# A sliding-window matmul: row blocks of w that shrink to 3, 2 and 1 rows per partition, the last two summed together, and a column-group tail of 4 k tiles

## The chip, the cores and the metric

One core of a Trainium2 chip runs the kernel. The metric is device time in microseconds (us), the median of several executions; the profile is one execution. "Span" is the time from the first to the last instruction of that execution, about 1.9 us less than its device time. All runs compared here are of the state "fast" unless it is said otherwise; a run is called slow when it takes over 1.5% longer than the fastest of the same kernel. Engines in the profile: PE (matmul), PEld (its weight load), DVE (vector), ACT (scalar), POOL (GpSimd, which here does little but issue DMAs), SP (sync).

## The reference

```python
# x: (4, 4096, 4096) fp32, w: (4096, 4096) fp32, offsets: 4 integers
for b in range(4):
    o = int(offsets[b])
    out[b] = x[b, o:o+64] @ w        # fp32 (4, 64, 4096)
```

Four windows of 64 rows make 256 rows, two groups (g = 0, 1) of 128. Each of the 4096 x 4096 weights is needed once: 67.1 MB of w, 4.2 MB of x, and 4.2 MB of result. A "k tile" is 128 rows of w, 2.10 MB; there are 32.

## The kernel before

w comes from HBM in fp32 and is cast to fp16 by the DMA on its way into the on-chip memory. Tiles 0 and 1 are loaded apart. Then come "row blocks": one transfer loads r tiles, and each partition gets r whole rows that lie side by side in w. Three buffers of 4 tiles each take turns. The last tiles are the "tail": they come in two column groups of 2048 columns, the second half of the columns first, so that one half of the result is complete, and can be stored, before all of w is there. A "run" is what a transfer reads in one piece for one partition: r rows of 16 KB in a row block, at most 8 KB in the tail. The matmuls add up in PSUM, the memory of eight "banks" that PE writes; adding a bank to the sums in acc is called an evacuation.

```python
    blocks = [(0, 1), (1, 1), (2, 4), (6, 4), (10, 4), (14, 4), (18, 3), (21, 3)]   # (first k tile, rows per partition)
    k_tail = 24
    n_fine = 2
    R_MAX = 4
    wc_pool = ctx.enter_context(tc.tile_pool(name="wc", bufs=3))
    ...
    for k0, r in blocks[2:]:
        t = wc_pool.tile([P, R_MAX * N], fp16, name="wc", tag="wc")
        nc.gpsimd.dma_start(
            out=t[:, : r * N],
            in_=w[k0 * P : (k0 + r) * P, :].rearrange("(p r) n -> p (r n)", r=r),
        )
    ...
    order = [1, 0]                                  # column groups: second half first
    for ng, st in zip(order, (steps, fine_steps)):  # steps: 2 tiles x 2048 columns each; fine_steps: the last piece cut in 3
        t = wc_pool.tile([P, R_MAX * N], fp16, name="wc", tag="wc")
        for ki, n, c0, c1 in st:
            nc.gpsimd.dma_start(...)                # runs of 8 KB in w
    ...
    whole_rows([0, 1], range(8), True)              # per block: sum its tiles in a PSUM bank, then add the bank to acc (DVE)
    for k0, r in blocks[2:-1]:
        whole_rows(range(k0, k0 + r), range(8), False)
    ...                                             # the last block: first column half alone here,
    ng = order[0]                                   # second half together with the tail
    kts = list(last_block) + list(range(k_tail, n_k))
    ...                                             # matmuls, then 4 adds on DVE, 4 copies on ACT and 4 adds of the copies
        store(nc.gpsimd, g, ng * NG, (ng + 1) * NG) # 1 MB each, two of them
    ng = order[1]
    ...                                             # the tail of the first half; stores of 512 KB each, two on ACT's queue, two on SP's
```

## Time and profile before

| | before |
|---|---|
| median (range) | 182.37 us (182.19 to 182.54, 6 runs) |
| span of the profile (that execution took 182.56 us, more than any of the six) | 180.6 us |
| PE, DVE, ACT busy | 125.7, 80.5, 16.5 us |
| moved by the DMAs over the span | 418 GB/s |
| last landing of w; last landing of a store | 169.81; 179.70 us |

The last row is from the trace's completion records, in which each of the 16 DMA engines tells when its share of a transfer is done; I give the time of the last of the 16.

### The profile page before, as it was taken

The page shows a single profiled execution, that of the slowest core. Times are in us where ns is not written, and L with a number is a line of the kernel's source. Part 1 is how long each engine was busy: PE and PEld are TensorE (multiplying, and loading weights), DVE is VectorE, ACT ScalarE, POOL GpSimd, SP SyncE. Part 2 cuts the span into 40 slices and gives each one's busy share as a digit, 9 for nine tenths or more (in the row PEclk, how much of TensorE's full clock was granted, in tenths as well). Part 3 has the DMA queues.
Part 4 walks back from the last instruction along what each step waited for, and adds up shares of the span by engine and source line. Part 5 has one row for each costly group of instructions (what it writes and reads, how often), then busy time and mean ns, then how long its engine had stood idle before and what let it go on. Part 6 is the DMA issues. An engine that isn't in the chain of part 4 may idle for free.

```text
span 180.6 us, 1505 instructions
## 1 busy us (share of the span) xinstructions
PE 125.7 (70%) x576; PEld 58.1 (32%) x576; DVE 80.5 (45%) x120; ACT 16.5 (9%) x23; POOL 14.5 (8%) x29
## 2 busy tenths in 40 slices
PE   0000779504999399808995699999399999987900
PEld 0000774101444144303442244444044444433400
DVE  0000657500578278802876168899374000820460
ACT  2412446500000000000000000000000000400000
POOL 4600000000000100000001000050500100020000
PEclk9999999965799999996999889999879999999996
DMA  5999989999999899999989989999999999999994
GB/s 178 321 256 212 281 181 196 236 232 232 225 218 218 174 210 234 236 218 232 210 181 203 245 191 245 194 239 196 191 212 213 215 216 214 212 216 206 370 419 196
DMA packets 4952, 40.98 MB, mean 227 GB/s; under 512 B 466, under 2 KB 466, under 8 KB 3282
## 3 DMA queue, kind: packets, MB, share of 16 engines
q0 software_dynamic: 4080, 36.70, 93.8%
q1 hardware_dynamic: 432, 2.10, 3.2%
q10 hardware_dynamic: 434, 2.10, 2.8%
q8 instruction: 4, 0.07, 0.1%
q14 instruction: 2, 0.02, 0.0%
HBM read 71.30 MB, written 4.19 MB: 418 GB/s over the span
## 4 chain that ended last, share of the span: by engine, by line
DMA 63%; PE 26%; issue 3%; DVE 2%; POOL 1%; POOLq 1%; DVEq 0%
DMA wc<-in_w_dram 63%; PE bank L144 26%; DVE acc L154 2%; POOL wc L108 1%; POOLq L70 1%; POOL xrow L77 0%; DVEq L251 0%; POOL identity masks.py:197 0%; POOLq L77 0%; POOL w L66 0%; POOLq masks.py:199 0%; DVEq L154 0%; POOLq L240 0%
## 5 line engine op out<-in xcount | busy, mean ns | idle before, releaser
L144 PE MATMUL bank<-wc,xT 128*128 128x512 f16 x480 | 111.6, 396 | 26.2 <-DMA wc<-in_w_dram 26.2
L154 DVE TENSOR_TENSOR acc<-acc,bank 128x512 f32<-128x512 f32 x100 | 67.0, 686 | 70.7 <-PE bank L144 70.0
L144 PEld LDWEIGHTS <-xT 128*128 128x128 f16 x512 | 51.5, 101 | 93.1 <-DMA wc<-in_w_dram 26.7
L130 PE MATMUL bank<-identity,xrow 128*128 128x128 f16 x64 | 7.1, 312 | 20.0 <-DMA xrow<-in_x_dram 20.0
L139 DVE CAST xT<-bank 128x512 f16<-128x512 f32 x8 | 5.5, 692 | 21.9 <-PE bank L130 21.9
L130 PEld LDWEIGHTS <-xrow 128*128 128x128 f16 x64 | 6.7, 149 | 20.2 <-issue 20.2
L200 ACT COPY tmp<-bank 128x512 f32<-128x512 f32 x4 | 2.1, 600 | 119.9 <-PE bank L144 119.9
L89 POOL DMA_DIRECT2D wc<-in_w_dram x6 | 3.2, 542 | 88.2 <-PE bank L144 88.2
L108 POOL DMA_DIRECT2D wc<-in_w_dram x10 | 6.7, 683 | 36.0 <-PE bank L144 26.4
L144 PE MATMUL bank<-w,xT 128*128 128x512 f16 x32 | 7.2, 382 | 0.0
L169 DVE COPY acc<-bank 128x512 f32<-128x512 f32 x8 | 5.5, 692 | 1.4 <-PE bank L144 1.2
L141 ACT CAST xT<-bank 128x512 f16<-128x512 f32 x8 | 4.7, 586 | 8.2 <-PE bank L130 8.2
L171 ACT COPY acc<-bank 128x512 f32<-128x512 f32 x8 | 4.7, 586 | 2.3 <-PE bank L144 2.3
L189 POOL DMA_DIRECT2D out_dram<-acc x2 | 1.1, 534 | 18.1 <-DVE acc L205 18.1
L205 DVE TENSOR_TENSOR acc<-acc,tmp 128x512 f32<-128x512 f32 x4 | 2.5, 681 | 0.0
L63 ACT CAST w<-acc 128x2048 f16<-128x2048 f32 x1 | 1.9, 1897 | 4.9 <-DMA acc<-in_w_dram 4.9
L77 POOL DMA_DIRECT2D xrow<-in_x_dram x4 | 2.1, 523 | 2.1 <-issue 2.1
L62 ACT CAST w<-acc 128x2048 f16<-128x2048 f32 x1 | 1.9, 1897 | 3.0 <-DMA acc<-in_w_dram 3.0
L62 ACT ACT_TABLE_LOAD x1 | 1.3, 1283 | 1.8 <-PEq L240 1.8
L66 POOL DMA_DIRECT2D w<-in_w_dram x1 | 0.7, 660 | 0.8 <-POOLq L240 0.8
masks.py:199 POOL TENSOR_SCALAR_AFFINE_SELECT identity<-identity 128x128 f16<-128x128 f16 x1 | 0.3, 287 | 0.1
masks.py:197 POOL MEMSET identity<- 128x128 f16 x1 | 0.2, 223 | 0.0
(4 smaller groups left out, 0.4 us busy)
## 6 DMA issues: line engine op xcount, KB each, us to landing
wc<-in_w_dram POOLq DMA_DIRECT2D x4, 4096.0 KB, 48.2
wc<-in_w_dram POOLq DMA_DIRECT2D x7, 1024.0 KB, 27.5
wc<-in_w_dram POOLq DMA_DIRECT2D x2, 3072.0 KB, 36.1
xrow<-in_x_dram POOLq DMA_DIRECT2D x4, 512.0 KB, 14.7
out_dram<-acc POOLq DMA_DIRECT2D x2, 1024.0 KB, 14.5
acc<-in_w_dram SPq DMA_DIRECT2D x1, 1024.0 KB, 5.3
w<-in_w_dram POOLq DMA_DIRECT2D x1, 1024.0 KB, 12.2
acc<-in_w_dram ACTq DMA_DIRECT2D x1, 1024.0 KB, 11.5
```

What stands on the lines that cost most here:

```text
L62: nc.scalar.copy(out=w_one[0][:, :NG], in_=w0_32[:, :NG])
L77: nc.gpsimd.dma_start(out=x16[g][m * WIN : (m + 1) * WIN, :], in_=x[b][bass.ds(o, WIN), :],)
L89: nc.gpsimd.dma_start(out=t[:, : r * N], in_=w[k0 * P : (k0 + r) * P, :].rearrange("(p r) n -> p (r n)", r=r),)
L108: nc.gpsimd.dma_start(out=t[:, pos : pos + n * wd].rearrange("p (t n) -> p t n", t=n), in_=w[ki * P : (ki + n) * P, ng * NG + c0 : ng * NG ...
L130: nc.tensor.matmul(out=ps[t][:, i * P : (i + 1) * P], lhsT=x_cols(g, 4 * t + i), rhs=identity[:], start=True, stop=True,)
L139: nc.vector.tensor_copy(out=dst, in_=ps[t][:])
L141: nc.scalar.copy(out=dst, in_=ps[t][:])
L144: nc.tensor.matmul(out=ps[bank][:], lhsT=xT[g][:, kt * P : (kt + 1) * P], rhs=rhs, start=start, stop=stop,)
L154: nc.vector.tensor_add(out=dst, in0=dst, in1=ps[bank][:])
L169: nc.vector.tensor_copy(out=acc[g][:, c * NT : (c + 1) * NT], in_=ps[bank][:])
L171: nc.scalar.copy(out=acc[g][:, c * NT : (c + 1) * NT], in_=ps[bank][:])
L205: nc.vector.tensor_add(out=dst, in0=dst, in1=tmp[2 * g + j // 2][:])
```

## The change

Its intent: the more of w comes as whole rows, the less comes in the short runs of the tail; and if the blocks get smaller towards the end, PE is left with less to do when the last block lands, so that a tail of only 4 tiles is enough to have half of the result stored in time. The blocks of 2 and 1 rows share one buffer and are summed together in PSUM (the "join", one evacuation instead of two), and the whole tail fits one buffer.

```diff
-    blocks = [(0, 1), (1, 1), (2, 4), (6, 4), (10, 4), (14, 4), (18, 3), (21, 3)]
-    k_tail = 24
+    blocks = [(0, 1), (1, 1), (2, 4), (6, 4), (10, 4), (14, 4), (18, 4), (22, 3), (25, 2), (27, 1)]
+    n_join = 2
+    k_tail = 28
...
+    free = 0
     for k0, r in blocks[2:]:
-        t = wc_pool.tile([P, R_MAX * N], fp16, name="wc", tag="wc")
+        if free < r:
+            t = wc_pool.tile([P, R_MAX * N], fp16, name="wc", tag="wc")
+            free = R_MAX
+        base = (R_MAX - free) * N
+        free -= r
...
+    t = wc_pool.tile([P, R_MAX * N], fp16, name="wc", tag="wc")
+    pos = 0
     for ng, st in zip(order, (steps, fine_steps)):
-        t = wc_pool.tile([P, R_MAX * N], fp16, name="wc", tag="wc")
-        pos = 0
...
-    for k0, r in blocks[2:-1]:
+    for k0, r in blocks[2:-n_join]:
         whole_rows(range(k0, k0 + r), range(8), False)
-    (first half of the last block with whole_rows)
+    join = range(blocks[-n_join][0], k_tail)
...
+    def columns(ng, kts):            # matmuls of kts for one column group, then the adds and copies as before
+        ...
+    columns(order[1], list(join))
     ng = order[0]
+    columns(ng, list(join) + list(range(k_tail, n_k)))
```

More of the change, by code (lines that the diff above doesn't have):

```diff
@@ L86 @@
     }
+    free = 0
     for k0, r in blocks[2:]:
-        t = wc_pool.tile([P, R_MAX * N], fp16, name="wc", tag="wc")
+        if free < r:
[3 more added lines that the diff above has]
+        free -= r
         nc.gpsimd.dma_start(
-            out=t[:, : r * N],
+            out=t[:, base : base + r * N],
             in_=w[k0 * P : (k0 + r) * P, :].rearrange("(p r) n -> p (r n)", r=r),
@@ L93 @@
         for q in range(r):
-            src[k0 + q] = lambda a, e, t=t, c=q * N: t[:, c + a : c + e]
+            src[k0 + q] = lambda a, e, t=t, c=base + q * N: t[:, c + a : c + e]
     tail = {}
@@ L173 @@
     whole_rows([0, 1], range(8), True)
-    for k0, r in blocks[2:-1]:
+    for k0, r in blocks[2:-n_join]:
         whole_rows(range(k0, k0 + r), range(8), False)
-    k0, r = blocks[-1]
-    last_block = range(k0, k0 + r)
-    whole_rows(last_block, range(order[1] * n_sub, (order[1] + 1) * n_sub), False)
+    join = range(blocks[-n_join][0], k_tail)
     def tail_mm(ki, g, ng, j, start, stop):
@@ L189, in store @@
             eng.dma_start(out=out_rows[g * P + a : g * P + e, c0:c1], in_=acc[g][a:e, c0:c1])
-    ng = order[0]
-    kts = list(last_block) + list(range(k_tail, n_k))
-    for ki in kts:
-        for g in range(G):
-            for j in range(n_sub):
-                tail_mm(ki, g, ng, j, ki == kts[0], ki == kts[-1])
-    for g in range(G):
-        for j in range(0, n_sub, 2):
-            add_out(4 * g + j, g, ng * n_sub + j)
-            nc.scalar.copy(out=tmp[2 * g + j // 2][:], in_=ps[4 * g + j + 1][:])
-    for g in range(G):
-        for j in range(1, n_sub, 2):
-            c = ng * n_sub + j
-            dst = acc[g][:, c * NT : (c + 1) * NT]
-            nc.vector.tensor_add(out=dst, in0=dst, in1=tmp[2 * g + j // 2][:])
+    def columns(ng, kts):
+        for ki in kts:
+            for g in range(G):
+                for j in range(n_sub):
+                    tail_mm(ki, g, ng, j, ki == kts[0], ki == kts[-1])
+        for g in range(G):
+            for j in range(0, n_sub, 2):
+                add_out(4 * g + j, g, ng * n_sub + j)
+                nc.scalar.copy(out=tmp[2 * g + j // 2][:], in_=ps[4 * g + j + 1][:])
+        for g in range(G):
+            for j in range(1, n_sub, 2):
+                c = ng * n_sub + j
+                dst = acc[g][:, c * NT : (c + 1) * NT]
+                nc.vector.tensor_add(out=dst, in0=dst, in1=tmp[2 * g + j // 2][:])
+    columns(order[1], list(join))
+    ng = order[0]
+    columns(ng, list(join) + list(range(k_tail, n_k)))
+    for g in range(G):
         store(nc.gpsimd, g, ng * NG, (ng + 1) * NG)
```

## The prediction

> **What bounds the kernel now.** I read the page of the kernel before in this order: the bytes, the row of busy slices, the chain that ended last, then the timeline from 60 us on.
>
> ```profile
> span 180.6 us, 1505 instructions
> ...
> DMA  5999989999999899999989989999999999999994
> ...
> HBM read 71.30 MB, written 4.19 MB: 418 GB/s over the span
> ...
> DMA wc<-in_w_dram 63%; PE bank L144 26%; DVE acc L154 2%; POOL wc L108 1%; POOLq L70 1%; POOL xrow L77 0%; DVEq L251 0%; POOL identity masks.py:197 0%; POOLq L77 0%; POOL w L66 0%; POOLq masks.py:199 0%; DVEq L154 0%; POOLq L240 0%
> ```
>
> The DMA row never falls below 8 between the first slice and the last. The whole span, start and end included, moves 71.30 + 4.19 = 75.49 MB at 418 GB/s. PE is busy 70% (and its modelled matmuls flatter it), DVE 45%. The 26% of the chain that is put on PE is not a bound by itself; it must be asked whether DMA was idle meanwhile. The stretches of the trace say no (columns: PE, PEld, DVE, ACT, POOL busy; clock; DMA share; GB/s written by the DMAs, where the weights count half, as they turn from fp32 into fp16 on the way):
>
> ```profile
> 60.00:80.00 20.00, 13.99 (x64) 6.19 (x64) 11.03 (x17) 0.00 (x0) 0.60 (x2) 1.00 0.98 211
> 145.00:165.00 20.00, 18.07 (x84) 8.03 (x82) 4.89 (x8) 2.06 (x4) 1.07 (x2) 1.00 1.06 213
> 165.00:175.00 10.00, 6.91 (x32) 2.94 (x30) 4.87 (x8) 0.00 (x0) 0.00 (x0) 1.00 1.05 353
> ```
>
> So 211 to 213 GB/s written means some 422 to 426 GB/s read. The timeline gives the pace, because PE or the issuing engine starts as each piece lands:
>
> ```profile
> 62.31 13.99 PE L144 MATMUL bank<-wc,xT 128*128 128x512 f16 x64 [3.07 <-DMA wc<-in_w_dram]
> ...
> 81.75 15.62 PE L144 MATMUL bank<-wc,xT 128*128 128x512 f16 x64 [5.46 <-DMA wc<-in_w_dram]
> ...
> 101.13 26.03 PE L144 MATMUL bank<-wc,xT 128*128 128x512 f16 x112 [3.76 <-DMA wc<-in_w_dram]
> ...
> 117.10 2.83 POOL L108 DMA_DIRECT2D wc<-in_w_dram  x4 [18.90 <-PE bank L144]
> 127.47 2.12 POOL L108 DMA_DIRECT2D wc<-in_w_dram  x3 [7.54 <-PE bank L144]
> 130.18 29.12 PE L144 MATMUL bank<-wc,xT 128*128 128x512 f16 x128 [3.02 <-DMA wc<-in_w_dram]
> ...
> 158.35 0.54 POOL L189 DMA_DIRECT2D out_dram<-acc  x1 [17.45 <-DVE acc L205]
> ...
> 164.84 7.07 PE L144 MATMUL bank<-wc,xT 128*128 128x512 f16 x32 [1.27 <-DMA wc<-in_w_dram]
> ...
> 172.08 2.72 SPq L189 DMA_DIRECT2D out_dram<-acc  x2
> ```
>
> A k tile is 128 rows of w, 2.10 MB. Between the landings at 62.31 and 130.18 lie the row blocks of 4, 4, 3 and 3 tiles: 67.87 / 14 = **4.85 us a tile**. Between 130.18 and 164.84 lie seven tail pieces of the size of one tile: 34.66 / 7 = **4.95 us**. One piece's worth is left after 164.84 (the fine pieces), about 5.0 us, so w ends near 169.8. Then 4.19 MB of stores at 418 GB/s take 10.0 us: 179.8. The span ends at 180.6. The end is thus the end of a queue of bytes that never runs dry, and not the chain from the last matmul: all the stores stand behind the last piece of w whatever PE does, so long as they are issued in time.
>
> **What the Trainium skill says.** (1) "DMA: Bandwidth & Descriptors", section Issuing engines are not separate DMA queues: DMAs of all issuing engines run on the same 16 engines and interleave. The trace agrees: its completion records have the four last stores (512 KB each, issued from two engines) land 1.25 us apart, one after the other, at 419 GB/s in all. (2) The same page, section Bandwidth, Measured: 425 GB/s for one 16 MB load, with a ceiling of 435 that it puts on the SBUF side. Here the reads run at 422 to 426 with only half the bytes on the SBUF side; so I take the figure as the limit of what can be read, and there is no large reserve. The page's fixed 2 us a DMA is not seen between queued DMAs, whose landings lie 4.85 or 4.95 us apart. (3) "TensorE: Matmul & The Clock Gate", section HAM oscillation: PE gaps of over some 3.4 us return the clock to half. The trace agrees: 64 matmuls take 13.99 us after a 3.07 us gap (the stretch from 60 to 80 shows a clock of 1.00) and 15.62 us after one of 5.46.
>
> **The change part by part.**
> Bytes: none removed or added. The blocks become 4,4,4,4,4,3,2,1 instead of 4,4,4,4,3,3, and the tail in column groups falls from 8 tiles to 4. Four tiles move from 4.95 to 4.85 us: 4 x 0.10 = **0.4 us earlier**. If the 2- and 1-row blocks run only at the tail's pace, 3 x 0.10 of that is lost.
>
> Evacuations: before, 5 blocks x 16 + 8 + 4 + 8 = 100 adds out of PSUM, 4 adds from tmp, 4 copies. After, 6 x 16 + 4 + 4 + 8 = 112, 8 and 8. DVE gets 12 x 0.686 + 4 x 0.681 = 11.0 us more, ACT 4 x 0.60 = 2.4 us. All of it lies beside transfers, except two changes of column group where banks must come free. The matmuls stay at 512.
>
> Buffers: the fifth block still waits for the first buffer in turn; the blocks of 2 and 1 share one buffer, and the whole tail shares the next. Predicted landings at 4.85 a tile from 101.1: block (18,4) 120.5; (22,3) 135.0; (25,2) 144.7; (27,1) 149.6; tail A, second group's columns, 154.5 and 159.5; tail B 164.4; the fine pieces to 169.4. The issue of (25,2) and (27,1) waits for the matmuls of (14,4), near 117 as now; the queue then holds until 135.0. The issue of all tail pieces waits for the matmuls of (18,4): 120.5 + 15.6 = 136.1; the queue holds until 149.6. So 13 us to spare: DMA doesn't run dry.
>
> PE: from 120.5 on it has 64 matmuls (15.6 us with the cold start, to 136.1), 48 for (22,3) at 0.217 us (to 146.5), 24 for the join's first group (to 151.9, as (27,1) lands at 149.6), then, once banks are free, 56 of the second group, then 32 of the last. At the switch DVE frees a bank in 0.69 us and ACT in 0.60, four each: 2.8 us for eight banks, of which 1.5 us lie under the last matmuls of the join and 1.7 beside the next ones: a stall of some 0.5 us, twice. So the second group ends at 152.4 + 12.2 = 164.6 (before: 155.7), and all matmuls at 165.1 + 7.0 = 172.1 (before: 171.9). PE has nearly no rest from 120.5 on, whereas before it caught up with the DMA at 159.3.
>
> Stores: the first two were issued 2.7 and 3.9 us after the end of the second group (155.7 to 158.35 and 159.56); they come at 167.3 and 168.5, instead of 11 us ahead of the end of w now only 1 to 2 us ahead of 169.4. Still in time. They give the DMA 5 us of work, to 174.4, and the first half of the last group is stored from about 171.1 on. The last store needs its turn near 178 and is issued near 174.8. So the end is again the queue: 169.4 + 10.0 + 0.8 = 180.2, and the sum is **0.4 us less**: 182.35 - 0.4 = **181.95 us**.
>
> **The rivals.**
> (a) PE becomes the bound. For it: 224 matmuls in one run of 51 us ending with the DMA; if the clock stays cold longer or a bank wait is longer, stores come late and DMA idles. Against it: about 1 us of slack at the first store, and 2 to 3 us at the last. Two further us on PE would cost about 1 us: 183.
> (b) A buffer wait takes the place of the DMA's flow, as one buffer now holds all of the tail and its issue is bound to the block of 4 ahead. Against it: 13 us. If it ran dry, each us adds a us; 185 would need that margin to be wrong by 16.
> (c) Smaller blocks have shorter runs (16 KB a partition at one row against 64 KB) and lose pace. The tail's rows are read in runs of 8 KB and lose only 2%; so at most some 0.3 us: 182.3.
> (d) The gain is larger, because the tail of 8 was the part that hurt. At most 0.10 x 8 = 0.8 us is there in all, and over 2% (3.65 us) would need 427 GB/s over the whole span, its start and end included. Nothing shows that.
>
> **Range and chances.** 0.4 us of gain, with (c) taking up to 0.3 and (a) up to 1 us back, and 0.1 us between runs: 181.2 to 183.2. Faster by over 2% is 178.7 or less: 0.02. Slower by over 2%, 186.0 or more, needs (a) and (b) together or something unseen: 0.04. Within 2%: 0.94.
>
> **What would show it.** In the profile after: 418 to 419 GB/s over the span, the DMA row full as before; 112, 8 and 8 evacuations; PE starting (18,4) near 120.5 and going on nearly without a wait to 172; the group stores issued near 167 and 169; the last landing near 179.3. I am wrong if the DMA row shows a gap near 135 to 150 (b), or one after 169 with stores issued later than 170 (a), or if the landings of the 2- and 1-row blocks lie over 5 us a tile apart (c).

## The result, and the profile after

The changed kernel takes **182.12 us** (182.01 to 182.31, 6 runs) against 182.37 us. The ratio is 0.9987, with a 95% interval of 0.9974 to 1.0. A ratio here is the mean time of one kernel's fast runs over that of the other's fast runs of the same rounds, so not quite the ratio of the medians. The change is worth a quarter of a microsecond, at the edge of what six runs can tell from nothing.

From the page of the changed kernel: span, DMA row, bytes, the chain by engine, and the three groups of evacuations (operation, shapes, count, then busy us and mean ns, then the idle time ahead).

```profile
span 180.2 us, 1537 instructions
...
DMA  5999989999998899999989999989999999999995
...
HBM read 71.30 MB, written 4.19 MB: 419 GB/s over the span
...
DMA 58%; PE 30%; issue 3%; DVE 2%; another core or an unknown queue 1%; POOL 1%; POOLq 1%; DVEq 0%
...
L160 DVE TENSOR_TENSOR acc<-acc,bank 128x512 f32<-128x512 f32 x112 | 75.2, 687 | 61.5 <-PE bank L150 60.9
...
L203 ACT COPY tmp<-bank 128x512 f32<-128x512 f32 x8 | 4.1, 599 | 127.5 <-PE bank L150 127.5
...
L208 DVE TENSOR_TENSOR acc<-acc,tmp 128x512 f32<-128x512 f32 x8 | 5.0, 682 | 0.0
```

The DMA row is as full as before and the rate over the span is 419 instead of 418 GB/s. The evacuations are 112, 8 and 8 as counted beforehand; DVE is busy 90.6 us instead of 80.5, and the time didn't notice. From the timeline of the changed kernel (start, length, what, and in brackets the idle time ahead of it and what ended it):

```profile
120.43 43.22 PE L150 MATMUL bank<-wc,xT 128*128 128x512 f16 x192 [2.61 <-DMA wc<-in_w_dram]
...
136.32 3.92 POOL L114 DMA_DIRECT2D wc<-in_w_dram  x6 [17.14 <-PE bank L150]
...
164.42 7.08 PE L150 MATMUL bank<-wc,xT 128*128 128x512 f16 x32 [0.77 <-DMA wc<-in_w_dram]
...
166.15 0.54 POOL L193 DMA_DIRECT2D out_dram<-acc  x1 [25.91 <-DVE acc L208]
```

PE runs from 120.43 to 163.65 without a break, waits 0.77 us for the DMA, and ends at 171.50. The first store of the finished half is issued at 166.15, where before it was 158.35. The landings, from the completion records, beside what was predicted for them (us):

| | predicted | measured |
|---|---|---|
| (18,4), (22,3) | 120.5, 135.0 | 120.39, 134.85 |
| (25,2), (27,1) | 144.7, 149.6 | 144.75, 149.46 |
| tail, second half of the columns | 154.5, 159.5 | 154.58, 159.47 |
| tail, first half; end of w | 164.4; 169.4 | 164.38; 169.36 |
| last store | 179.3 | 179.27 |

The end of w came 0.45 us earlier than before (169.81), and so did the last store (0.43). These are two single executions, and the one of the kernel before (182.56 us) is slower than all six that were timed, the one of the changed kernel (182.01) the fastest of its six; so a part of the 0.45 is the spread between executions.

### The profile page after: what moved, and what is told of

It is laid out like the page before. It is cut to its first block, busy times and chain, and to the rows that moved or that the text cites. A ratio compares the mean times of both kernels' runs of the same rounds, so it can differ in the third digit from the quotient of the medians.

```text
span 180.2 us, 1537 instructions
## 1 busy us (share of the span) xinstructions
PE 127.2 (71%) x576; PEld 57.0 (32%) x576; DVE 90.6 (50%) x136; ACT 18.3 (10%) x27; POOL 12.7 (7%) x27
## 4 chain that ended last, share of the span: by engine, by line
DMA 58%; PE 30%; issue 3%; DVE 2%; another core or an unknown queue 1%; POOL 1%; POOLq 1%; DVEq 0%
DMA wc<-in_w_dram 58%; PE bank L150 30%; DVE acc L160 2%; POOL wc L114 1%; POOLq L71 1%; POOL xrow L78 0%; DVEq L259 0%; POOL identity masks.py:197 0%; POOLq L78 0%; POOL w L67 0%; POOLq masks.py:199 0%; POOLq L248 0%
## 5 line engine op out<-in xcount | busy, mean ns | idle before, releaser
L150 PE MATMUL bank<-wc,xT 128*128 128x512 f16 x480 | 115.0, 405 | 24.3 <-DMA wc<-in_w_dram 24.3
L160 DVE TENSOR_TENSOR acc<-acc,bank 128x512 f32<-128x512 f32 x112 | 75.2, 687 | 61.5 <-PE bank L150 60.9
L150 PEld LDWEIGHTS <-xT 128*128 128x128 f16 x512 | 52.1, 103 | 93.8 <-DMA wc<-in_w_dram 27.2
L136 PE MATMUL bank<-identity,xrow 128*128 128x128 f16 x64 | 5.3, 258 | 20.0 <-DMA xrow<-in_x_dram 20.0
L203 ACT COPY tmp<-bank 128x512 f32<-128x512 f32 x8 | 4.1, 599 | 127.5 <-PE bank L150 127.5
L95 POOL DMA_DIRECT2D wc<-in_w_dram x8 | 4.3, 540 | 108.1 <-PE bank L150 108.1
L136 PEld LDWEIGHTS <-xrow 128*128 128x128 f16 x64 | 5.0, 124 | 20.1 <-issue 20.1
L114 POOL DMA_DIRECT2D wc<-in_w_dram x6 | 3.9, 674 | 17.1 <-PE bank L150 17.1
L208 DVE TENSOR_TENSOR acc<-acc,tmp 128x512 f32<-128x512 f32 x8 | 5.0, 682 | 0.0
```

Source lines behind the costliest of these rows:

```text
L95: nc.gpsimd.dma_start(out=t[:, base : base + r * N], in_=w[k0 * P : (k0 + r) * P, :].rearrange("(p r) n -> p (r n)", r=r),)
L114: nc.gpsimd.dma_start(out=t[:, pos : pos + n * wd].rearrange("p (t n) -> p t n", t=n), in_=w[ki * P : (ki + n) * P, ng * NG + c0 : ng * NG ...
L136: nc.tensor.matmul(out=ps[t][:, i * P : (i + 1) * P], lhsT=x_cols(g, 4 * t + i), rhs=identity[:], start=True, stop=True,)
L150: nc.tensor.matmul(out=ps[bank][:], lhsT=xT[g][:, kt * P : (kt + 1) * P], rhs=rhs, start=start, stop=stop,)
L160: nc.vector.tensor_add(out=dst, in0=dst, in1=ps[bank][:])
L203: nc.scalar.copy(out=tmp[2 * g + j // 2][:], in_=ps[4 * g + j + 1][:])
```

## The experiments

All outputs are right. Each job also ran the kernel before on its chip; its medians were 182.35, 182.27 and 182.31 us in the three jobs, so that the times below can be held against the 182.12 us of the changed kernel to about 0.1 us. Each edit is one of the changed kernel. My theory was that the time is the length of a queue of bytes, and that the change shortens it a little because its last tiles are read in longer runs; what PE does is hidden so long as the stores come in time.

### Does the layout of the reads cost anything, and is it the runs or the number of transfers?

**e1_col_halves**: every row block is loaded as two column halves, so in runs of 8 KB, with 8 transfers more.

```diff
+        for h in range(2):
             nc.gpsimd.dma_start(
-                out=t[:, base : base + r * N],
-                in_=w[k0 * P : (k0 + r) * P, :].rearrange("(p r) n -> p (r n)", r=r),
+                out=t[:, base : base + r * N].rearrange("p (r n) -> p r n", r=r)[:, :, h * NG : (h + 1) * NG],
+                in_=w[k0 * P : (k0 + r) * P, h * NG : (h + 1) * NG].rearrange("(p r) n -> p r n", r=r),
             )
```

> The changed kernel, but every row block (k tiles 2 to 27) is loaded as two column halves, so that all of w behind tile 1 is read in runs of 8 KB like the tail. Theory (the time is the queue of bytes, and runs of 8 KB cost 0.10 us a tile): 26 tiles x 0.10 = 2.6 us more than the changed kernel, 184.7 us, landings of a block of 4 tiles 19.8 us apart instead of 19.37. Rival 1 (what costs is the number of transfers, 0.10 us for each of the tail's): 8 transfers more, 182.9. Rival 2 (the 0.25 us of gain is chance and the layout of the reads costs nothing): 182.1.

Measured: 183.81 us (183.67 to 183.85), 1.69 more than the changed kernel; the end of w and the last store both 1.65 us later in the trace. So the layout of the reads does cost time, but the size fits neither 2.6 nor 0.8. The 22 tiles behind the landing of the first block came every 4.92 us (43.21 to 151.34) instead of every 4.84 (43.06 to 149.46). So a tile costs 0.08 and not 0.10 us, and the first block, which landed within 0.15 us of the other's, hardly adds.

**e2_row_parts**: every block of several rows is loaded as two transfers split by rows, 7 transfers more, with whole rows in each.

```diff
-        nc.gpsimd.dma_start(
-            out=t[:, base : base + r * N],
-            in_=w[k0 * P : (k0 + r) * P, :].rearrange("(p r) n -> p (r n)", r=r),
-        )
+        cuts = [0, (r + 1) // 2, r] if r > 1 else [0, 1]
+        for a, e in zip(cuts, cuts[1:]):
+            nc.gpsimd.dma_start(
+                out=t[:, base + a * N : base + e * N].rearrange("p (r n) -> p r n", r=e - a),
+                in_=w[k0 * P : (k0 + r) * P, :].rearrange("(p r) n -> p r n", r=r)[:, a:e, :],
+            )
```

> The changed kernel, but every row block of more than one row per partition is loaded as two transfers split by rows, so that the number of transfers rises by 7 but runs stay whole rows (16 KB and more). Theory (length of runs): 182.1 us, within 0.2. Rival 1 (number of transfers): about 182.8. If this is slow and the column halves are not, the theory falls.

Measured: 182.83 us (182.67 to 182.94), 0.71 more, and the end of w 0.59 us later (169.95). Here the rival's figure came out, not mine. But the runs got shorter too (2 rows side by side instead of 4), so that this run alone does not name the cause.

**e8_short_runs**: the same transfers as in the changed kernel, but a gap of 16 elements behind every 2048 columns of the buffer, so that no run is longer than 8 KB. In the trace, the packets of the row blocks (each is one record in the trace) shrink from 8 to 32 KB written, depending on r, to 4 KB.

```diff
-            t = wc_pool.tile([P, R_MAX * N], fp16, name="wc", tag="wc")
+            t = wc_pool.tile([P, R_MAX * (N + 32)], fp16, name="wc", tag="wc")
...
-            out=t[:, base : base + r * N],
-            in_=w[k0 * P : (k0 + r) * P, :].rearrange("(p r) n -> p (r n)", r=r),
+            out=t[:, base : base + r * (N + 32)].rearrange("p (c n) -> p c n", n=NG + 16)[:, :, :NG],
+            in_=w[k0 * P : (k0 + r) * P, :].rearrange("(p r) (h n) -> p (r h) n", r=r, h=2),
...                       # base, the tail's buffer and the matmuls' column ranges follow the gaps
```

> The changed kernel, same number of transfers and same order of w in the buffer, but every row block is written into pieces of 2048 columns with a gap of 16 elements between them, so that no run is longer than 8 KB read and 4 KB written. Theory (length of runs is the cost): as with the column halves less the cost of their 8 more transfers: 183.1 us; if all of the column halves' 1.7 us is run length: 183.8. Rival (number of transfers): 182.1.

Measured: 183.28 us (183.23 to 183.38), 1.16 more, and the end of w 1.32 us later (170.68); 4.89 us a tile. The number of transfers is unchanged, so this part is the length of the runs: 0.05 us a tile. Column halves cost 0.53 us more than this at the same run length with 8 transfers more, which would be 0.07 us a transfer. The landings give less: w ends only 0.33 us later in e1 than in e8 (171.01 against 170.68), 0.04 us a transfer. The spans differ by more because of what comes after the last landing: 1.29 us in e1 and 1.43 in e2, where POOL sits idle for some 0.4 us among the program's closing instructions, against 0.91 in all other runs. That isn't the DMA queue, and its cause isn't shown. By the landings, then, about four fifths of e1 is the runs (1.32 of 1.65 us), by the times two thirds.

**e9_rows_apart**: the same transfers, but the rows of a partition are 128 apart in w, so that every run is one row of 16 KB. The columns of x follow (second part of the edit).

```diff
-            out=t[:, base : base + r * N],
-            in_=w[k0 * P : (k0 + r) * P, :].rearrange("(p r) n -> p (r n)", r=r),
+            out=t[:, base : base + r * N].rearrange("p (r n) -> p r n", r=r),
+            in_=w[k0 * P : (k0 + r) * P, :].rearrange("(r p) n -> p r n", p=P),
...
-        for k0, r in blocks:
-            if k0 <= kt < k0 + r:
-                a = k0 * P + kt - k0
-                return x16[g][:, a : a + r * (P - 1) + 1 : r]
```

> The changed kernel, same number of transfers, but a partition's rows are 128 apart in w instead of side by side, so that every run is one row of 16 KB (the x columns are taken without stride to fit). Theory (below 16 KB a run costs, above it nothing, as the landing of the 1-row block 4.71 us after the block ahead suggests): 182.1 us, within 0.2. Rival (rows side by side, runs of 64 KB, are what makes the blocks fast): 182.6 or more.

Measured: 182.53 us (182.39 to 182.57), 0.41 more, of which 0.24 us are there at the end of w (169.60). Neither expectation is met exactly. In its profile the store of the finished half also came late (issued at 167.69), so a part of the 0.41 is of the kind of the next section; what remains for runs of 16 KB is some 0.24 us in 26 tiles, by one trace. It also helps with e2, whose runs were no shorter than these but whose w ended 0.59 us late: about 0.35 us of that is left for its 7 transfers, 0.05 us each. So a transfer more in the queue costs some 0.04 us (e1 against e8) to 0.08 us (if all of e2's 0.59 were put on its transfers).

**e6_old_tail**: one part of the change alone, blocks that shrink (3, 2, 1 rows) and are summed together, with the old tail of 8 tiles in two buffers.

```diff
-    blocks = [..., (14, 4), (18, 4), (22, 3), (25, 2), (27, 1)]
-    k_tail = 28
+    blocks = [..., (14, 4), (18, 3), (21, 2), (23, 1)]
+    k_tail = 24
...
-    t = wc_pool.tile([P, R_MAX * N], fp16, name="wc", tag="wc")
-    pos = 0
     for ng, st in zip(order, (steps, fine_steps)):
+        t = wc_pool.tile([P, R_MAX * N], fp16, name="wc", tag="wc")
+        pos = 0
```

> One part alone: shrinking blocks summed together (3, 2 and 1 rows), but the tail in column groups of 8 tiles as before. Theory (the gain is four tiles read in longer runs): as the kernel before, 182.35 us, within 0.2; the eight tail tiles at 4.95 us each again. Rival (the gain is the earlier start of the last sums): 182.1. By time alone the two are at the edge of what five rounds resolve; the landings decide.

Measured: 182.31 us (182.06 to 182.48), ratio to the kernel before 0.9997 (0.9984 to 1.001); w ends at 169.76. No gain of shrinking the blocks by themselves is seen. By time it is not told apart from the changed kernel with certainty (the intervals of the two ratios overlap). The landings, which I had said would decide, don't quite: the end of w, 169.76 against 169.81 and 169.36, sides with the theory, but the profiled execution is the slowest of its five (182.48), and the eight tail tiles came every 4.91 us (130.50 to 169.76), not every 4.95.

### How much time has PE?

**e3_plus8** and **e4_plus24**: matmuls whose result is thrown away, ahead of the second half's sum.

```diff
     ng = order[0]
+    for _ in range(1):               # e4_plus24: range(3)
+        for g in range(G):
+            for j in range(n_sub):
+                tail_mm(join[0], g, ng, j, True, True)
     columns(ng, list(join) + list(range(k_tail, n_k)))
```

> The changed kernel with 8 matmuls more (thrown away, the result stays right) ahead of the second group's sum, 1.75 us of PE right on the chain that the profile calls the last one. Theory (queue of bytes, PE has slack): the group's stores are issued near 167.9 and 169.1, before w ends at 169.4, and the last store still waits for its turn: 182.1 us, within 0.3. Rival (the chain through PE, DVE and the last store sets the end): 0.8 us of PE's wait is used up, the rest is seen: 183.1.

> The same with 24 matmuls more, 5.2 us of PE. Theory: the slack is used up; the group's stores are issued at about 171.4 and 172.6, two to three us after w has ended, and the DMA row shows a hole there: 185 us (184.2 to 186.2). Rival (the chain): 5.2 less the 0.8 us of wait: 186.5. If PE did not matter at all: 182.1.

Measured: 182.92 us (182.43 to 184.06) and 186.10 us (186.07 to 187.21). Both are nearer to the rival's figures than to mine, though e4_plus24 lies within the range that I gave. The trace of e4_plus24 shows why. Stretches of that kernel (start:end, length, then busy time and count of PE, PEld, DVE, ACT, POOL, then clock, DMA share, GB/s written):

```profile
167.00:169.00 2.00, 2.00 (x11) 0.94 (x10) 1.60 (x3) 1.39 (x3) 0.00 (x0) 1.00 0.56 103
169.00:170.00 1.00, 1.00 (x6) 0.41 (x5) 1.00 (x3) 0.67 (x2) 0.00 (x0) 1.00 0.00 0
170.00:171.00 1.00, 1.00 (x6) 0.49 (x5) 1.00 (x3) 0.00 (x0) 0.00 (x0) 1.00 0.00 0
171.00:172.00 1.00, 1.00 (x7) 0.45 (x5) 1.00 (x3) 0.00 (x0) 0.54 (x1) 1.00 0.00 0
172.00:173.00 1.00, 1.00 (x6) 0.44 (x5) 0.29 (x1) 0.00 (x0) 0.42 (x1) 1.00 0.63 262
```

The same stretches of the changed kernel:

```profile
167.00:169.00 2.00, 2.00 (x11) 0.92 (x10) 0.06 (x1) 0.00 (x0) 0.53 (x1) 1.00 1.10 331
169.00:170.00 1.00, 1.00 (x6) 0.46 (x5) 0.84 (x2) 0.00 (x0) 0.00 (x0) 1.00 1.09 459
```

With 24 matmuls more, w is through at 169 and the DMA engines then move nothing for three microseconds (share 0.00) until the store of the finished half is issued, at 171.38. Its first packet starts at 172.49. The hole of some 3.7 us (168.76 to 172.49) is what the run is slower by, 4.0 us: the queue, and not the 5.2 us of PE, sets the end. How late may the store be? From issue to first packet it takes 1.11 us, in this run and in e3_plus8 (169.37 to 170.48) and e5 below (169.43 to 170.54) alike. And the 16 DMA engines do not finish w together: in the changed kernel the quickest takes its first packet of the store at 167.41, the slowest its last packet of w at 169.02. To leave none idle, the store must be issued by 166.3. It is issued at 166.15. But it costs little if only the quicker engines stand idle, as all traces together show (from the completion records, us; "lead" is from the issue of the first store to the last landing of w):

| | lead | last landing of w to last landing of a store |
|---|---|---|
| before, e6, e1, e8, changed kernel, e10, e2 | 11.46, 13.54, 3.72, 3.25, 3.21, 2.90, 2.50 | 9.88 to 9.92 |
| e9 | 1.91 | 10.03 |
| e7 | 1.52 | 10.44 |
| e3, e5 | -0.05, -0.11 | 12.00, 12.05 |
| e4 | -2.34 | 14.30 |

With a lead of 2.5 us or more the stores take 9.9 us behind w. Below some 2.05 us (an estimate from the last four rows, which agree on it within 0.02), each us of lead that is missing costs about one us. The changed kernel's lead of 3.21 us thus leaves about 1.2 us of slack, where the kernel before had over 9.

The spread of e3_plus8 has a cause of its own: four of its six runs took 182.43 to 182.95 and two took 184.0. The profiled one is of the slow two (184.06), and the block (18,4) has kept PE longer in it; the tail is issued as this block's matmuls end. From its timeline:

```profile
137.81 3.92 POOL L114 DMA_DIRECT2D wc<-in_w_dram  x6 [19.40 <-PE bank L150]
...
169.37 0.54 POOL L193 DMA_DIRECT2D out_dram<-acc  x1 [27.65 <-DVE acc L208]
```

137.81 instead of 136.32. Two stretches of e3_plus8, then the same two of the changed kernel, show where it went (the granted clock is the third number from the end):

```profile
122.00:124.00 2.00, 2.00 (x6) 0.70 (x5) 0.69 (x1) 0.00 (x0) 0.00 (x0) 0.50 0.97 209
124.00:126.00 2.00, 2.00 (x6) 0.76 (x5) 0.69 (x1) 0.00 (x0) 0.00 (x0) 0.50 0.97 209
```

```profile
122.00:124.00 2.00, 2.00 (x7) 0.71 (x6) 0.71 (x2) 0.00 (x0) 0.00 (x0) 0.57 0.91 197
124.00:126.00 2.00, 2.00 (x11) 0.94 (x10) 1.65 (x3) 0.00 (x0) 0.00 (x0) 1.00 1.09 233
```

The clock was at 0.50 for over two microseconds longer after the wait ahead of this block, with 6 matmuls in place of 11 in the second stretch. The store is late by this and by the 8 matmuls. I have no profile of a run of the other kind, so for these the sum is an estimate: issued at 167.9, a lead of 1.5 us where 2.05 are needed, so about 0.55 us more; the four took 0.57 us more on average than the changed kernel.

**e5_one_last_block**: the tail of 4, but tiles 25 to 27 as one block.

```diff
-    blocks = [..., (18, 4), (22, 3), (25, 2), (27, 1)]
-    n_join = 2
+    blocks = [..., (18, 4), (22, 3), (25, 3)]
+    n_join = 1
```

> The changed kernel with its tail of 4, but the tiles 25 to 27 come as one block of 3 rows instead of 2 and 1. Theory (the time is the queue of bytes, as long as the second group's stores are issued 1.6 us before w ends[...]): PE must wait for 149.5 with three tiles to sum instead of one, is 3.3 us later (up to 4.8 if its clock has fallen), the stores are issued at 169.5 to 171, a hole of 1.7 to 3.2 us opens: 184.5 us (183.6 to 185.5). Rival (only the shorter tail matters, the shrinking blocks do nothing): 182.1.

Measured: 183.97 us (four runs within 183.95 to 183.97, one at 185.58; one at 186.97 was slow). Within the range expected, and 1.85 us slower than the changed kernel. The lead of 1.6 us that the expectation asks for was too short by the table above. From its timeline:

```profile
149.48 24.35 PE L150 MATMUL bank<-wc,xT 128*128 128x512 f16 x112 [2.94 <-DMA wc<-in_w_dram]
...
169.43 0.54 POOL L193 DMA_DIRECT2D out_dram<-acc  x1 [29.04 <-DVE acc L208]
```

PE waits 2.94 us for three tiles at once and the store is issued at 169.43 instead of 166.15. So this is what the blocks of 2 and 1 rows are for: not for speed of their own (e6), but to let a tail of 4 be short without the store coming late.

**e10_no_fine**: an attempt to beat both kernels; the last two tiles of the last half come as one transfer and not as three.

```diff
-    for ng, st in zip(order, (steps, fine_steps)):
+    for ng, st in zip(order, (steps, steps)):
```

> An attempt at a faster version: the changed kernel with the last two tiles of the last group as one transfer instead of three finer ones, two transfers fewer. Theory: the last matmuls come 1.3 us later but the last store has its turn only near 178, so PE's delay is hidden; two transfers less are worth 0.05 to 0.1 us each: 182.0 us, within 0.2. Rival (the fine pieces are there because the last matmuls set the end): 183.3.

Measured: 182.26 us (182.09 to 182.35), ratio to the kernel before 0.9995 (0.9982 to 1.0009): the same as the changed kernel, no gain. Its timeline is of more use than its time:

```profile
169.27 3.61 PE L150 MATMUL bank<-wc,xT 128*128 128x512 f16 x16 [1.28 <-DMA wc<-in_w_dram]
...
173.06 2.73 SPq L193 DMA_DIRECT2D out_dram<-acc  x2
```

The matmuls end at 172.88 instead of 171.50 and SP starts to issue its stores 1.4 us later (173.06 against 171.67), and yet the last store lands at 179.12 (179.27 in the changed kernel). The edit also takes two transfers away, but w ends only 0.13 us earlier with it (169.23), so that this cannot have hidden the 1.4 us. The very pieces that the chain of the page names as last, the closing matmuls and adds, may come 1.4 us later for nothing.

### What do the buffers hold up?

**e7_two_buffers**: two buffers for w instead of three.

```diff
-    wc_pool = ctx.enter_context(tc.tile_pool(name="wc", bufs=3))
+    wc_pool = ctx.enter_context(tc.tile_pool(name="wc", bufs=2))
```

> The changed kernel with two buffers for w instead of three. Theory (the third buffer is what keeps the queue of bytes full): the blocks of 2 and 1 can then only be issued when the matmuls of (18,4) have ended, 136.0, with the first byte 1.1 us later, while (22,3) has landed at 134.9 (the fastest engines are done 1.4 us earlier): a hole of 2.3 to 3.7 us there and none elsewhere, 184.4 to 186.0 us, a dip of the DMA row near 135. Rival (the waits for buffers are far from the path, 13 us to spare, and it changes nothing): 182.1.

Measured: 190.15 us (189.02 to 191.49), about 8 us more; I had reckoned with one hole of 2.3 to 3.7 us. The profile is of the slowest of its four runs (191.49), with the last store 9.4 us late. The hole is where it was expected, but it is larger, and it is not the only loss. From its timeline, and two of its stretches (columns as above):

```profile
118.66 0.53 POOL L95 DMA_DIRECT2D wc<-in_w_dram  x1 [19.00 <-PE bank L150]
...
123.41 26.46 PE L150 MATMUL bank<-wc,xT 128*128 128x512 f16 x112 [5.05 <-DMA wc<-in_w_dram]
139.81 1.06 POOL L95 DMA_DIRECT2D wc<-in_w_dram  x2 [20.62 <-PE bank L150]
```

```profile
134.00:138.00 4.00, 4.00 (x20) 1.81 (x19) 3.12 (x6) 0.00 (x0) 0.00 (x0) 1.00 0.35 74
138.00:142.00 4.00, 4.00 (x20) 1.83 (x19) 3.65 (x6) 0.00 (x0) 1.06 (x2) 1.00 0.43 61
```

The DMA share falls to 0.35 and 0.43. What I left out is that delays add up: with two buffers, block (10,4) already landed 1.4 us late, (14,4) 1.6 and (18,4) 3.0 us late (123.36), so the matmuls that free the buffer ended later too, and the blocks of 2 and 1 rows were issued at 139.81 and not at 136.3. With the third buffer none of this is seen. Sharing a buffer between two blocks, and one for the whole tail, thus cost the change nothing only because a buffer was in reserve.

## Why the prediction was right

- *What bounds the kernel.* Right. The predicted end of w, of the last store and the span agree with the trace to 0.05 us, and holding up DMA (e4, e5, e7) shows in the time, while 10 us more of DVE and 1.4 us more of PE at the end (e10) do not. That the agreement is to 0.05 us is in part luck: the profile is of the fastest of six executions, and by the median the forecast of 181.95 was 0.17 us too low.
- *Four tiles from 4.95 to 4.85 us, 0.4 us earlier.* Right in kind: e1 and e8 with short runs for all tiles cost 1.7 and 1.2 us, and e6 without the shorter tail shows no gain, though it alone decides nothing. As to size, the end of w moved by 0.45 us, and the medians by 0.25. The dearer tile is not of one cause: 0.05 us is the length of the runs. That the rest goes with the number of transfers (one a tile in the tail, one for four tiles in most blocks) fits their 0.04 to 0.08 us, but is reckoned and not shown.
- *The 2- and 1-row blocks may run at the tail's pace (rival c).* They came 14.61 us after the block ahead, 4.87 us a tile, nearly at the pace of the others.
- *Evacuations.* 112, 8 and 8, hidden, as worked out.
- *Buffers: 13 us to spare (rival b).* The tail was issued at 136.32 while the queue lasted until 149.46, so this holds for three buffers; e7 shows what it is without the reserve.
- *PE.* The two stalls of 0.5 us for banks did not occur: 128 matmuls from 136.03 to 163.65 took 0.216 us each, so none of them waited. So the second half was ready at 163.65 instead of 164.6 and the store came at 166.15 instead of 167.3.
- *"Still in time", "about 1 us of slack at the first store" (rival a).* Right in what came of it, but by two errors that cancelled each other, and that is luck. At the predicted issue of 167.3 the lead would have been 2.1 us, of which some 2.05 are needed: no slack at all, though no cost yet. I had left out the 1.11 us from issue to first packet, and that the quicker engines are through with w 1.6 us before the slowest. But the store came 1.15 us earlier than forecast, mostly for the stalls that did not occur, and so the slack is about the 1 us that I gave. The price of 2 us more on PE, 183 us, is about right: e3 took 182.92 for 1.75 us, and 182.70 in the mean of its four quicker runs.
- *"The trace agrees" on the clock (point 3 of what the Trainium skill says).* This reading was too quick. It holds for the two waits named, but the line of 130.18 that is shown above it has a wait of only 3.02 us, and its 128 matmuls took 29.12 us, 0.227 each instead of the 0.219 after the wait of 3.07; the stretch from 130 to 135 has a clock of 0.71. In the changed kernel the clock fell after a wait of 2.61 us too (0.57 in the stretch 122 to 124 shown above). So here the length of the wait alone does not tell. The prediction's 15.6 us for block (18,4) reckoned with a cold start all the same and came out (120.43 to 136.03).
- *2 to 3 us of slack at the last store.* At least 1.4 us of it is shown by e10.

What stays open: why runs of 8 KB cost 1% of the pace, and why a transfer that waits in a queue costs some 0.04 to 0.08 us at all. No run tells where in the DMA this is lost. How the DMA engines come to end 1.6 us apart isn't shown either.

## What to carry to other kernels

When the DMA row is full from end to end and bytes over span equals the pace of a single transfer, add up bytes first: such a kernel can only be changed by what the bytes cost each (runs, number of transfers) and by holes. The chain that ended last is then no list of what to shorten; ask of each of its pieces whether something else was in the queue meanwhile, and test it by making that piece longer. A store that is to follow loads without a hole must be issued well ahead of the last load's landing: here by 2.05 us, more than the 1.11 us from issue to first packet; the quickest engine ran out of loads 1.6 us before the slowest. Measure this lead in several runs before calling a slack used up.

## What the Trainium skill lacked or had wrong

- "DMA: Bandwidth & Descriptors", section Specifications, gives 512 B as the least transfer for line rate. With a cast from fp32 to fp16, runs of 8 KB were still slower than the blocks' runs of up to 64 KB: 4.89 against 4.84 us for 2.10 MB (e8), 1.16 us in the whole kernel.
- The same page, section Bandwidth, has HBM bind a load at some 358 GB/s and puts the ceiling of 435 on the ports of the on-chip memory. Its own 425 GB/s for 16 MB, taken with the pair's other core idle, stands beside them. This core read at 2.10 MB / 4.84 us = 434 GB/s, while it wrote only half of that, because of the cast. So the first figure is no bound here, and the second fits a load that casts although the ports then carry half of it; the page says nothing of this case.
- The same page, section Anatomy of one DMA, has a fixed cost of 2 us a DMA. For a transfer behind others in the queue, the runs show 0.04 us (e1 against e8, at the end of w) to 0.08 us (e2). Its first-byte figure of about 1 us for transfers issued by GpSimd agrees: 1.11 us from issue to first packet in three runs. I found no page that gives how far apart the engines end a stream of loads (1.6 us, 167.41 to 169.02, in the changed kernel), or how far ahead of the last landing the next transfer must be issued to cost nothing (2.05 us here).
